# Moving eight conditioning vectors of layer 0 from the mixer's stretch to the second MLP product

## The chip, the cores and the metric

One core of a Trainium2 chip runs the whole program. The metric is the device time of one execution in microseconds (us), the median of several runs. Five engines work beside each other, each in the order of its own instruction list: TensorE (PE, products), VectorE (DVE), ScalarE (ACT), GpSimd (POOL) and SyncE (SP), which here issues every DMA transfer.

## The reference, cut to what matters

The model has two layers over 1024 latent and 128 context tokens. Each layer takes six vectors per conditioning (there are two conditionings) from one product with `w_mod`, uses two of them to scale and shift the input of the mixer, one (`g1`) to scale the mixer's result, two for the MLP's input and the last (`g2`) to scale the MLP's result:

```python
sh1, sc1, g1, sh2, sc2, g2 = ada_modulation(cond, p['w_mod'], p['b_mod'])
h = rms_norm(x, p['norm1']) * (1 + sc1) + sh1
...
x = x + g1 * mix
h2 = rms_norm(x, p['norm2']) * (1 + sc2) + sh2
x = x + g2 * (jnp.square(jax.nn.relu(h2 @ p['w1'])) @ p['w2'])
```

`ada_modulation` is `silu(cond) @ w_mod + b_mod`, a vector of 6 x 1024 numbers, which the kernel cuts into 48 tiles of 128: tiles 0 to 15 are `sh1` and `sc1`, 16 to 23 `g1`, 24 to 39 `sh2` and `sc2`, 40 to 47 `g2`.

## The kernel before, in words

Activations stand feature by feature (128 features on the partitions, tokens along the row). The program goes, for each layer, through these stages, one after the other but overlapping at the edges:

- the norm and the first input projections (in layer 0 with tiles 0 to 15 of its own vectors);
- the mixers A and B: first the RG-LRU (`rglru`, line 719, two halves of 15 steps), then the HGRN2 recurrence (`HGRN`, line 493, two head pairs of three chunks with seven levels each). Both are long chains of small operations on DVE, ACT and POOL with few products. PE fills the time with input projections, which are the "side" of each weave (lines 1477 to 1484);
- the neighbourhood attention with the rest of the projections, and the output projection;
- the first MLP product (W1) and the second one (W2, lines 1758 to 1891). W2 is done in eight groups of 8 units (`order`, `line.add`, line 1843); a unit is seven block products in a Strassen-like form, whose results DVE adds from PSUM to rows in SBUF (`second`, line 1797). POOL, ACT and DVE also cut weights and operands into a high and a low part.

A **mod tile** (`mod_tile`, line 276) makes one of the 48 tiles for both conditionings. It loads 128 x 1024 weights from `w_mod` in pieces, as wide as the buffer it is given, and has DVE multiply each piece with the silu of the conditioning and sum it along the row, once for each conditioning (line 286; the trace shows the reduction and a short read of its accumulator as two instructions). Given a buffer of 384 columns a tile takes three pieces, 3 DMAs and 6 reductions; given one of 1152 columns it takes one piece, 1 DMA and 2 reductions of 1024 columns. Tiles 8 to 15 and 32 to 39 have one short instruction more (line 292).

In layer 0 the tiles 16 to 47 are made beside the mixers: `MODS[0]`, 10 of them, between the steps of the RG-LRU, in buffers of the mixers' pool of 28 (`g_`), and `MODS[1] + MODS[2]`, 22, between the steps of HGRN2, in a pool of four buffers (`sqt`); `left` (line 1452) hands out the numbers in order. Layer 1's tiles are made under W2: 40 of them under layer 0's W2 and 8 under its own (`later`, line 1784), spread evenly over units 2 to 44 of the 64 (`MODS2`, line 51), in buffers of 1152 columns (`hr_`). `g2` is first read in the seventh group of W2, where `combine` (line 1819) multiplies by `mod[l][:, 40 + k]`.

The order on each engine is not written out: a scheduler runs a model of the program and lets each engine take the ready instruction of the highest priority. Priority follows the place in the program; the recurrences get 300 places of advance (`RG_AHEAD`, `HG_AHEAD`), the mod tiles none. An instruction that needs a buffer is ready when the buffer is free. On the chip each engine then follows the order that came out.

Of the kernel before, what the change touches and what calls it, by code (L numbers as in the profile page):

```python
# [64 lines left out]
def weave(main, n_main, side, n_side):  # L65

    done = [0, 0]
    gens = [main, side]
    n = [max(n_main, 1), max(n_side, 1)]
    live = [True, True]  # L70
    while live[0] or live[1]:
        i = 0 if live[0] and (not live[1] or done[0] * n[1] <= done[1] * n[0]) else 1
        try:
            next(gens[i])
            done[i] += 1
        except StopIteration:
            live[i] = False


def weave_steps(main, n_main, side, n_side):  # L80

    done = 0
    for i in range(n_main):
        if next(main, END) is END:
            return
        while done * n_main < (i + 1) * n_side and next(side, END) is not END:
            done += 1
        yield
    yield from main
# [20 lines left out]
def chain(*gens):  # L110
    for g in gens:
        yield from g
# [10 lines left out]
def build(ctx, tc, I, O):  # L123
# [9 lines left out]
    def urgent(gen, offset):  # L133

        while True:
            with tc.high_priority(offset):
                step = next(gen, END)
            if step is END:
                return
            yield step  # L140
# [106 lines left out]
    def load_cond(c):  # L247
        dma(sil[:, c], I["cond"][c:c + 1].to_broadcast([P, DM]))
        act(sil[:, c], sil[:, c], AF.Silu)
# [233 lines left out]
        return (M_BQ if what == "q" else M_BG) + p, e  # L483


    MODS = (10, 11, 11, 0)

    SIDE = 12 + 18 + 18
    HG_SIDE = 44
# [215 lines left out]
    def hgrns(pairs):  # L705

        rest, n = iter(()), 0
        for r in pairs:
            for g in range(NCH):
                yield from weave_steps(r.levels(g), r.LEVELS, rest, n)  # L710
                run_out(rest)
                rest, n = r.tail(g), r.TAIL
            rest, n = chain(rest, r.back()), r.TAIL + r.BACK
        yield from rest
# [94 lines left out]
    def qk_project(l, p, win, ht, qd, kd, s_, ns=range(NCH)):  # L809
        sub = vsub if p > 1 else psub  # L810
        h_t, l_t = s_("qh", F32R), s_("ql", F32R)
        yield from project(win(M_CQ + p), ht, lambda n, ps: split_q(ps, n, h_t, l_t, sub), ns)
        for j, t in enumerate((h_t, l_t)):
            for h in range(2):
                for o in range(2):
                    dma(qd[:, :, o, 2 * j + h].rearrange("t p c -> p t c"),
                        t[h * HD:(h + 1) * HD].bitcast(F32).rearrange("p (t c) -> p t c", c=P))

        def evac_k(n, ps):

            u, a, b = ft("ku"), ft("kh", F32R), ft("kl", F32R)
            w = NW if n < NCH - 1 else NW - TP
            acopy(u[:, :w].rearrange("p (i c r) -> p i r c", r=2, c=64), ps[:, :w].rearrange("p (i r c) -> p i r c", r=2, c=64))
            if n == NCH - 1:
                acopy(u[:, w:], ps[:, w:])
                dma(O["ck"][l, p * P:(p + 1) * P], u[:, w:])
            acopy(a, u)
            sub(b, u, a)
            for j, t in enumerate((a, b)):
                dma(kd[:, j, cs(n)], t.bitcast(F32))  # L830
        yield from project(win(M_CK + p), ht, evac_k, ns)
# [480 lines left out]
    for l in range(DEPTH):  # L1312
# [130 lines left out]
        def hp(p, w):  # L1443
            m, e = hgrn_evac(l, p, bp[p], w)
            return project(win(m), ht, e)

        def mods(n, piece):
            for j in take(left, n):
                mod_tile(0, j, piece)
                yield  # L1450

        left = iter(range(16, 48 if l == 0 else 16))

        def evac_vb(i, ps):
            n, j = divmod(i, 3)
# [5 lines left out]
        def v_project(g):  # L1461
            c = slice(g * 2 * P, (g + 1) * 2 * P)

            def e(i, ps):
                s = ft("vs")[:, :2 * P]
                (acopy if i % 2 else vcopy)(s, ps)
                if i < NC - 1:

                    dst = vd[ti(i), c].rearrange("(c r) m -> r c m", r=2)
                    for r in range(2):  # L1470
                        dma(dst[r], s[r * 64:(r + 1) * 64])
                else:
                    dma(vd[TS:, c], s)
                    dma(O["cv"][l][:, c], s)
            return project_tokens(l, 1 + g, ht, e, s_)

        side = chain(project_tokens(l, 0, ht, evac_vb, s_), *(hp(0, w) for w in "fbqg"))
        weave(weave_steps(urgent(chain(*(rglru(l, i, xa[i], gel[i], gw, ud, g_) for i in range(2))), RG_AHEAD), 2 * RG_STEPS,
                          mods(MODS[0], g_), MODS[0]), 2 * RG_STEPS, side, 21)
        side = chain(*(hp(1, w) for w in "fbqg"), *(v_project(j) for j in range(2)),  # L1480
                     *(qk_project(l, p, win, ht, qd[p], kd[p], s_) for p in range(3)))
        n = sum(MODS[1:3])
        weave(weave_steps(urgent(hgrns([HGRN(l, p, bp[p], ud, g_) for p in range(2)]), HG_AHEAD), HG_STEPS, mods(n, sqt), n), HG_STEPS,
# [153 lines left out]
        last = l + 1 == DEPTH  # L1637
# [95 lines left out]
        n = 0  # L1733
# [47 lines left out]
            run_out(group_operands(s))  # L1781
        for c in range(2):
            load_cond(c)
        later = iter([(1, j) for j in (range(40, 48) if last else range(40))])
        n_later, n = (8 if last else 40), 0

        rows = [row_("row") for _ in range(KD)]
        xs = [row_segs(r) for r in rows]
# [221 lines left out]
```

## Time and profile before

| what | value |
|---|---|
| median of 3 runs | 3277.85 us (3276.06 to 3279.03) |
| the profiled execution, its own time | 3276.47 us |
| its span, first to last instruction | 3274.7 us |
| granted TensorE clock over the span | 0.950 of full speed |
| PE busy | 2960.4 us, 90% of the span |
| DVE busy | 2406.1 us, 73% |
| ACT busy | 1641.4 us, 50% |
| POOL busy | 1567.8 us, 48% |
| moved by DMA | 566.48 MB, mean 173 GB/s |

The span is what lies between the first and the last instruction of the profiled execution; the execution's own time is 1.8 us more. Busy shares are averages over stages that have different limits, so a stage has to be looked at by itself. The two layers run the same code with the same shapes, but for the mod tiles: layer 1 makes none in its mixers and 8 instead of 40 in its W2. So each stage of layer 1 shows what that of layer 0 would be with fewer of them.

### The profile page before, as it was taken

The page shows a single profiled execution, that of the slowest core. Times are in us where ns is not written, and L with a number is a line of the kernel's source. Part 1 is how long each engine was busy: PE and PEld are TensorE (multiplying, and loading weights), DVE is VectorE, ACT ScalarE, POOL GpSimd, SP SyncE. Part 2 cuts the span into 40 slices and gives each one's busy share as a digit, 9 for nine tenths or more (in the row PEclk, how much of TensorE's full clock was granted, in tenths as well). Part 3 has the DMA queues.
Part 4 walks back from the last instruction along what each step waited for, and adds up shares of the span by engine and source line. Part 5 has one row for each costly group of instructions (what it writes and reads, how often), then busy time and mean ns, then how long its engine had stood idle before and what let it go on. Part 6 is the DMA issues. An engine that isn't in the chain of part 4 may idle for free. (4 is left out here: it accounts for less than half of the span.)

```text
span 3274.7 us, 61327 instructions
## 1 busy us (share of the span) xinstructions
PE 2960.4 (90%) x21208; PEld 2815.3 (86%) x21208; DVE 2406.1 (73%) x5283; ACT 1641.4 (50%) x4079; POOL 1567.8 (48%) x1528
## 2 busy tenths in 40 slices
PE   7888998998889998988868999999987999899995
PEld 7878888798789998888858889988977999899994
DVE  8899974667885568998874677346779755777787
ACT  5543234565566666344454533345646566654443
POOL 4541132345676665554545311334556765654453
PEclk8989999999899998999979999999998999999997
DMA  7342447983455567675522102689634655855552
GB/s 270 91 108 87 132 121 224 283 269 103 158 176 185 177 212 279 216 245 198 181 94 74 58 29 80 183 239 293 220 127 148 194 179 181 281 204 173 185 194 68
DMA packets 391318, 566.48 MB, mean 173 GB/s; under 512 B 45920, under 2 KB 250848, under 8 KB 391008
## 3 DMA queue, kind: packets, MB, share of 16 engines
q1 hardware_dynamic: 391008, 562.57, 53.8%
q8 instruction: 167, 2.74, 0.4%
q14 instruction: 143, 1.17, 0.1%
HBM read 397.01 MB, written 165.42 MB: 172 GB/s over the span
## 5 line engine op out<-in xcount | busy, mean ns | idle before, releaser
L189 POOL TENSOR_TENSOR wl<-wr,wh 128x512 fp32r<-128x512 f32 x164 | 231.1, 1413 | 485.4 <-ACT wh L186 379.2
L189 POOL TENSOR_TENSOR wt<-wl,wt 128x256 fp32r<-128x256 f32 x276 | 258.0, 942 | 176.5 <-ACT wt L186 116.5
L1110 PE MATMUL bB<-R,wt 128*128 128x288 f32 x768 | 236.9, 309 | 63.7 <-ACT bB L186 40.8
L189 POOL TENSOR_TENSOR ws<-wl,ws 128x512 fp32r<-128x512 f32 x160 | 227.5, 1426 | 121.4 <-ACT ws L186 121.3
L421 PE MATMUL pj<-hh,wh 128*128 128x384 f32 x640 | 223.7, 354 | 27.0 <-ACT g L213 12.3
L1110 PE MATMUL bB<-t,ws 128*128 128x288 f32 x768 | 231.7, 302 | 18.0 <-DVE hr L198 9.6
L423 PE MATMUL pj<-hh,wl 128*128 128x384 f32 x640 | 225.1, 352 | 7.1 <-POOL wl L189 7.1
L1111 PE MATMUL bB<-R,wt 128*128 128x288 f32 x768 | 231.1, 301 | 0.0
L1112 PE MATMUL bB<-R,wt 128*128 128x288 f32 x768 | 230.0, 300 | 0.0
L1111 PE MATMUL bB<-t,ws 128*128 128x288 f32 x768 | 229.6, 299 | 0.0
L1112 PE MATMUL bB<-t,ws 128*128 128x288 f32 x768 | 229.2, 299 | 0.0
L422 PE MATMUL pj<-hh,wh 128*128 128x384 f32 x640 | 223.4, 350 | 0.0
L1110 PEld LDWEIGHTS bB<-R,wt 128*128 128x128 f32 x768 | 148.2, 193 | 74.2 <-ACT bB L186 48.3
L186 ACT CAST wt<-wl 128x256 fp32r<-128x256 f32 x288 | 115.9, 406 | 159.8 <-PE bB L1112 82.0
L421 PE MATMUL wo<-u,wh 128*128 128x288 f32 x512 | 160.1, 314 | 17.1 <-DVE x L210 13.4
L1110 PEld LDWEIGHTS bB<-t,ws 128*128 128x128 f32 x768 | 147.6, 192 | 22.0 <-DVE hr L198 11.4
L186 ACT CAST wh<-wr 128x512 fp32r<-128x512 f32 x164 | 101.1, 618 | 129.3 <-PE pj L422 65.2
L207 POOL TENSOR_SCALAR pl<-pl,rc 128x384 f32<-128x384 f32 x128 | 79.1, 618 | 176.5 <-DVE rc L952 83.9
L1110 PE MATMUL bA<-R,wt 128*128 128x288 f32 x512 | 156.0, 305 | 8.1 <-DVE row L210 5.8
L1112 PE MATMUL bA<-t,ws 128*128 128x288 f32 x512 | 155.4, 304 | 8.0 <-DVE ws L192 6.5
L1110 PE MATMUL bA<-t,ws 128*128 128x288 f32 x512 | 155.1, 303 | 4.3 <-ACT ws L186 2.3
L1111 PE MATMUL bA<-R,wt 128*128 128x288 f32 x512 | 154.6, 302 | 0.0
(363 smaller groups left out, 11364.9 us busy)
## 6 DMA issues: line engine op xcount, KB each, us to landing
wr<-in_w SPq DMA_DIRECT2D x304, 256.0 KB, 3.3
R<-od SPq DMA_DIRECT2D x96, 576.0 KB, 5.6
xb<-or SPq DMA_DIRECT2D x128, 288.0 KB, 4.2
wm<-in_w_mod SPq DMA_DIRECT2D x64, 512.0 KB, 5.6
od<-sil SPq DMA_DIRECT2D x96, 288.0 KB, 2.9
od<-pad SPq DMA_DIRECT2D x96, 288.0 KB, 3.1
wr<-in_w_in SPq DMA_DIRECT2D x104, 256.0 KB, 3.0
bi<-in_bias SPq DMA_DIRECT2D x96, 192.0 KB, 4.5
```

The lines of the kernel that those rows point to most:

```text
L186: nc.scalar.copy(out=out, in_=in_)
L189: nc.gpsimd.tensor_tensor(out=out, in0=a, in1=b, op=ALU.subtract)
L207: nc.gpsimd.tensor_scalar(out=out, in0=a, scalar1=s1, scalar2=s2, op0=op0, op1=op1)
L421: mm(ps, lhsT=wh(k), rhs=ah(k), start=k == first, stop=False)
L422: mm(ps, lhsT=wh(k), rhs=al(k), start=False, stop=False)
L423: mm(ps, lhsT=wl(k), rhs=ah(k), start=False, stop=k == last)
L1110: mm(ps, lhsT=w[:, 0, ti(i)], rhs=t[:, 0], start=start and i == 0, stop=False, skip_group_check=True)
L1111: mm(ps, lhsT=w[:, 0, ti(i)], rhs=t[:, 1], start=False, stop=False, skip_group_check=True)
L1112: mm(ps, lhsT=w[:, 1, ti(i)], rhs=t[:, 0], start=False, stop=i == n - 1, skip_group_check=True)
```

## The change

`MODS[0]` falls from 10 to 2, so in layer 0 only tiles 16 and 17 stand between the steps of the RG-LRU, and tiles 18 to 39 between those of HGRN2. Tiles 40 to 47 of layer 0, which are `g2`, go to the head of the list that W2 of layer 0 works off; that list now has 48 tiles over the same 42 units. Layer 1's program is untouched, and so are the due times.

```diff
-    MODS = (10, 11, 11, 0)
+    MODS = (2, 11, 11, 0)
...
-        left = iter(range(16, 48 if l == 0 else 16))
+        left = iter(range(16, 40 if l == 0 else 16))
...
-        later = iter([(1, j) for j in (range(40, 48) if last else range(40))])
-        n_later, n = (8 if last else 40), 0
+        later = iter([(1, j) for j in range(40, 48)] if last else [(0, j) for j in range(40, 48)] + [(1, j) for j in range(40)])
+        n_later, n = (8 if last else 48), 0
```

## Rows read from the trace of the kernel before

**Rows 1.** The page: engines over the whole span, and two of the 40 slices' lines.
```profile
PE 2960.4 (90%) x21208; PEld 2815.3 (86%) x21208; DVE 2406.1 (73%) x5283; ACT 1641.4 (50%) x4079; POOL 1567.8 (48%) x1528
...
PE   7888998998889998988868999999987999899995
...
DVE  8899974667885568998874677346779755777787
```

**Rows 2.** Windows by stage: start:end, length, busy of each engine (instructions), clock, DMA share.
```profile
117.30:480.30 363.00, 322.15 (x2282) 293.80 (x2283) 334.76 (x951) 138.05 (x307) 108.96 (x103) 0.95 0.37 102
480.30:794.80 314.50, 293.13 (x2259) 264.52 (x2259) 187.02 (x555) 165.94 (x510) 124.76 (x180) 0.96 0.74 224
...
1241.70:1602.30 360.60, 329.83 (x2345) 323.01 (x2345) 329.12 (x629) 165.62 (x414) 187.92 (x171) 0.97 0.67 227
...
1758.50:2058.90 300.40, 280.59 (x2067) 254.88 (x2065) 205.35 (x555) 127.12 (x278) 86.35 (x84) 0.96 0.18 50
2058.90:2402.80 343.90, 328.97 (x2475) 298.18 (x2477) 187.80 (x555) 179.79 (x541) 142.56 (x200) 0.99 0.75 224
...
2845.40:3170.40 325.00, 316.47 (x2327) 313.93 (x2327) 241.01 (x485) 165.29 (x411) 158.48 (x168) 0.99 0.58 198
```

**Rows 3.** Tiles gr and av, layer 0: ns min/median/max, first and last start.
```profile
L740 PE MATMUL gr<-xc,gw x24: 484/486/590, 117.3 to 184.5; 128*128 128x384 f32 x24
...
L992 PE MATMUL av<-ptc,vc x256: 272/273/476, 553.9 to 794.8; 128*64 128x128 f32 x128
```

**Rows 4.** Windows of line 286 alone (the mod tiles), DVE busy, layer 0.
```profile
100.00:420.00 320.00, 132.29 (x384) 0.95 0.37 106
...
1260.00:1540.00 280.00, 114.89 (x160) 0.96 0.66 224
```

**Rows 5.** Lines by form, DVE, 100 to 420 and 1240 to 1560 us: the reductions.
```profile
L286 DVE CUSTOM_DVE_ANT_0 junk<-wm,sil,ma 128x384 bf16<-128x384 f32 x64 | 47.2, 738 | 3.6 <-DMA wm<-in_w_mod 2.8
L286 DVE CUSTOM_DVE_ANT_0 junk<-wm,sil,ma 128x256 bf16<-128x256 f32 x64 | 38.8, 606 | 0.7
...
L286 DVE CUSTOM_DVE_ANT_0 jk<-wm,sil,par 128x1024 bf16<-128x1024 f32 x80 | 114.2, 1428 | 3.8 <-ACT sil L213 2.2 <-DMA wm<-in_w_mod 1.5
```

**Rows 6.** Windows inside the mixers: RG-LRU and most of HGRN2, layers 0 and 1.
```profile
117.30:234.00 116.70, 91.50 (x493) 82.72 (x493) 103.75 (x222) 55.55 (x100) 53.76 (x46) 0.91 0.35 85
234.00:424.00 190.00, 176.15 (x1367) 162.36 (x1368) 184.83 (x593) 58.73 (x142) 36.01 (x36) 0.97 0.36 111
...
1758.50:1859.00 100.50, 85.39 (x465) 77.39 (x465) 50.09 (x83) 56.36 (x101) 50.35 (x46) 0.93 0.14 34
1859.00:2003.00 144.00, 139.29 (x1087) 126.87 (x1088) 109.70 (x325) 50.70 (x124) 24.85 (x28) 0.96 0.18 56
```

**Rows 7.** Tiles wm and scA in layer 0, and DVE's timeline around 224 us.
```profile
L286 DVE CUSTOM_DVE_ANT_0 junk<-wm,sil,ma x128: 453/605/1669, 119.5 to 416.1; 128x384 bf16<-128x384 f32 x64, 128x256 bf16<-128x256 f32 x64
...
L541 DVE COPY_PREDICATED scA<-masks,sc x42: 568/584/598, 245.4 to 480.3; 128x384 f32<-128x384 uint8 x42
...
225.72 0.61 DVE L286 CUSTOM_DVE_ANT_0 junk<-wm,sil,par 128x384 bf16<-128x384 f32 x1
```

**Rows 8.** Waits of SP, 100 to 240 us: total, times, longest.
```profile
SPq L216 <- DVE mod L286: 13.1, 4, 9.7
```

**Rows 9.** W2 of layer 0 while its mod tiles run: window, PE's and ACT's waits.
```profile
1263.00:1530.00 267.00, 237.33 (x1662) 231.37 (x1661) 259.68 (x492) 114.03 (x288) 141.31 (x121) 0.96 0.67 228
...
PE bB L1110 <- ACT bB L186: 21.0, 15, 2.4
...
ACT bB L186 <- DVE row L198: 31.1, 23, 3.7
```

**Rows 10.** Tile xm, 1200 to 1700 us: the first readers of g2.
```profile
L210 DVE SCALAR_TENSOR_TENSOR row<-row,mod,xm x16: 338/1097/1682, 1567.5 to 1620.3; 128x128 f32<-128x128 f32 x8, 128x1024 f32<-128x1024 f32 x8
```

**Rows 11.** Lines by form, POOL: W2 of layer 0 (1263:1530), then layer 1 (2867:3071).
```profile
L189 POOL TENSOR_TENSOR wt<-wl,wt 128x256 fp32r<-128x256 f32 x80 | 89.6, 1132 | 30.3 <-ACT wt L186 23.9 <-DVE mod L286 2.7 <-DVE wt L192 2.1
...
L189 POOL TENSOR_TENSOR wt<-wl,wt 128x256 fp32r<-128x256 f32 x71 | 59.3, 838 | 57.9 <-ACT wt L186 34.3 <-DVE row L198 16.5 <-issue 2.3
```

## The prediction, made before the changed kernel was built

> **What bounds the kernel now.** I first read the page's busy shares and slices [rows 1]: PE is at 90% of the span, yet its digits fall to 8 and below in many slices; DVE is at 73%, but of the six slices in which it reaches 9 five lie in two stretches, slices 3 to 5 (164 to 409 us) and 17 and 18 (1310 to 1474 us). There layer 0's mod tiles run [rows 4]. So I cut the span into stages at events that both layers have and compared the layers [rows 2, 3]: the mixers from the first gate product to HGRN2's last masked copy, the attention up to its last value product, W2 from its first product to the last plain add of its block bA. What the reader is to see: layer 0's mixers take 363.0 us and layer 1's 300.4, 62.6 more for 32 mod tiles; the attention after them takes 314.5 against 343.9, 29.4 less; W2 takes 360.6 with 40 tiles and 325.0 with 8, 35.6 more. PE does about the same products in either W2 (2345 and 2327 records), but in layer 0's mixers it does 2282 against 2067: while DVE holds up the recurrence, PE runs ahead through the projections, and gets that back in the attention. The lasting price of the 32 tiles is 62.6 - 29.4 = 33.2 us.
>
> Then I asked in each stage whether DVE is full. In HGRN2 it is busy 184.83 of 190 us (97%), in the RG-LRU 103.75 of 116.7 (89%), against 50.09 of 100.5 and 109.70 of 144 in layer 1 [rows 6]. In W2, while the mod tiles run, it is busy 259.68 of 267 us (97%), and PE's longest wait is for ACT's copy to the bank bB, which itself waits for DVE's adds to the rows [rows 9]. Both places, the one the tiles leave and the one they go to, are bound by DVE.
>
> **The change, part by part.**
>
> *Eight tiles fewer in the mixers.* 32 tiles keep DVE busy for 132.29 us [rows 4], 4.13 each, so eight take 8 x 4.13 = 33.1 us of DVE, and 24 DMAs. SP waited 13.1 us in the RG-LRU for reductions that free a buffer [rows 8]; weight loads stand behind such a wait, so fewer of these transfers can only help there.
>
> How much comes back? At the recurrence's end I take 1:1: with DVE at 97% each microsecond less of DVE is one less of stage. This needs the later tiles to move forward into the RG-LRU. The text puts eight fewer there, but the tiles of HGRN2 may run ahead of their place: the last reduction starts at 416.1, while they are spread in the text to the end of HGRN2, whose last masked copy is at 480.3 [rows 7]. I expect them to fill the RG-LRU's idle DVE in the same way. The recurrence then ends 33 us earlier. Next in line is PE: it has run less far ahead, so part returns as projections left for the attention. Of 62.6 us layer 0 got back 29.4, so 33.2 / 62.6 = 0.53 lasts, and 0.53 x 33.1 = 17.5 us. The bounds: nothing is given back, 33.1; or each tile is worth the mean of 32, 8 x 33.2 / 32 = 8.3. Lower still is the rival below in which the tiles don't move forward. A loss here I exclude: no instruction is added.
>
> *Eight tiles more under W2.* 40 tiles take 114.89 us of DVE there [rows 4], 2.87 each, so eight cost 23.0 us; a tile is cheaper by 1.26 us because two reductions of 1024 columns (1428 ns) take the place of four of 384 and two of 256 (738 and 606 ns) [rows 5]. DVE is left 7.3 us idle in 267 [rows 9], most of it at the edges; I let 1 us be absorbed. PE has no other work in W2 to run ahead with: a bank must be added to its row before it is written again. So nothing is given back later, and I take 22 us. The bounds: by the mean over the 32 tiles by which the layers differ it would be 8 x 35.6 / 32 = 8.9 us; by POOL's part (next) 23 + 6 = 29. I am near the upper one, because the row that holds is the 97%, not the mean over tiles of which the first ones filled idle time.
>
> *POOL beside these reductions.* POOL's low-part subtractions of 128x256 take 1132 ns in layer 0's W2 and 838 in layer 1's [rows 11]: 80 x 0.294 = 23.5 us more of POOL, with about 65 reductions more beside it, some 0.36 us each. Sixteen reductions would add 5.8 us to POOL, which is busy 141.31 of 267 us [rows 9] and has that free. I count it at nothing; if the weights that it makes were late, PE would wait by those 6 us.
>
> The Trainium skill speaks against the change here (SBUF — State Buffer, Who interferes with whom): a DVE instruction with two inputs in SBUF and a GpSimd one that reads SBUF share a port, and the second one blocks until the first has ended. By that rule, with every one of the 16 reductions holding POOL for its 1.43 us and all of it reaching PE, the time would be 3282 + 23 = 3305. The trace agrees in direction [rows 11], but shows 0.36 us for each, which POOL's idle time covers, and so 3282.
>
> *Moved with it.* Eight DMAs of 512 KB (three pieces become one) pass to W2, in SP's queue and in the ring of buffers that also feeds the operands. The DMA engines are 0.67 busy there [rows 2], so 4.2 MB find room: nothing, and some us of operand wait if a buffer is late. `g2` is first read at 1567.5 [rows 10], after all mod tiles (their last reduction is before 1540 [rows 4]), and its tiles come first in the list: no new wait. Layer 1's 40 tiles follow within the same units.
>
> **The sum** against the profiled execution's own 3276.5 us: - 17.5 + 22 = 3281.0. The runs' median, 3277.85, is 1.4 above that execution, so 3282.4 us, slower by 0.14%. A measurement of this kernel can tell some 0.2%, 6.6 us, from no change: below 3271.3 is faster, above 3284.4 slower.
>
> **The rivals**, on the scale of the median.
>
> *1. W2 pays, the mixers hardly return: slower.* The place is HGRN2 from 234 us on. If the scheduler doesn't bring its tiles forward, RG-LRU with 2 tiles gets nearly as short as layer 1's: 8/10 of 116.7 - 100.5, 13 us. But tile 11 starts at 225.7 in the kernel before [rows 7], so about two of the 22 were done when HGRN2 began; now they would stand in it with DVE full, 8 to 10 us. 13 - 10 = 3, of which 0.53 lasts: 2 us. With 22 of W2 that is + 20, 3298. It decides as soon as fewer than about 4 tiles move forward. For: the priorities follow the text, and none of HGRN2's tiles ran before the first ten were done. Against: the ten left no room, and later the tiles did run ahead. 0.2.
>
> *2. The mixers return all: faster.* The tail of the DVE-full stretch is what the last tiles cost; if 24 tiles leave PE as little idle as layer 1's mixers do (19.8 us against 40.9 [rows 2]), nothing is given back: - 33.1 + 22, 3266.8. For: the price per tile must rise with their number, and 33.2 us are just eight tiles at 4.13. Against: layer 1's attention is 29.4 us longer. 0.17.
>
> *3. W2 costs its mean price only:* - 17.5 + 8.9, 3269.3. Against: DVE's 97%. 0.05.
>
> *4. POOL becomes W2's bound,* and the weights' low parts come late: + 6, 3288. For: it is slowed already. Against: before these subtractions it is idle for 30.3 us, mostly waiting for ACT [rows 11]. 0.13. The Trainium skill's port rule (SBUF — State Buffer, Who interferes with whom) would make this rival likelier and dearer, up to the 3305 above, which the 0.36 us don't bear out.
>
> *5. The change doesn't do what it says:* the scheduler rearranges so much that the places of the tiles don't matter. 0.03, anywhere in the range.
>
> **How the numbers follow.** The likeliest case, 17.5 back and 22 paid, has 0.42 and gives 3282. Within 0.2% are it, nearly all, and little else: 0.42 in all, as what it loses at its edges it gets from the others. Slower: rivals 1 and 4 and a share of 5, 0.36. Faster: rivals 2 and 3, 0.22. For 8 in 10 the range goes from a little under rival 2, 3264, to rival 1, 3298; it takes in both bounds of the mixers with 22 paid (3267 and 3291.6) and leaves out only combinations of two extremes. The likeliest case alone would lie between 3274 (25 back, halfway to the upper bound, and 22 paid) and 3288 (13 back, halfway to the mean price, and 23 paid).
>
> **What would show it.** In the changed profile: reductions on buffers of 384 columns 144 instead of 192, busy near 99 us; reductions of 1024 columns 112 instead of 96. The mixers' stage near 330 us and the attention's near 330, with the last small reduction near 383; W2's near 383, with DVE at 97% or more while its tiles run and PE still waiting for the copy to bB. Wrong would be: a mixers' stage that stays over 350 (rival 1), an attention that stays at 315 (rival 2), a W2 under 372 (rival 3) or PE waiting for POOL's weights in it (rival 4).

## The result and the profile after

The changed kernel takes 3300.11 us (median of 6 runs, 3291.68 to 3301.31) against 3276.06 us of the kernel before in the same set: 1.0079 of it, 95% interval 1.0066 to 1.0093, so 26 us slower by this ratio (24 by the two medians). That is outside the predicted range, 2 us above its upper end, and 18 us above the predicted time. The profiled execution took 3298.01 us, its span is 3296.2 us.

The page of the kernel after, the lines that answer to [rows 1]:

```profile
PE 2966.8 (90%) x21208; PEld 2818.2 (85%) x21208; DVE 2405.4 (73%) x5219; ACT 1646.8 (50%) x4083; POOL 1563.7 (47%) x1528
...
PE   7888999999799988888869899999987999899995
...
DVE  8799864577975578999893587345778755777787
```

DVE's total is the same within a microsecond, though eight tiles now cost 22 us where they cost 33: other DVE instructions became longer. Its slices show where the tiles went: the fifth and sixth fell from 9 and 7 to 8 and 6, and the 9s of W2 now reach from the 17th to the 19th, one more than before.

The windows of the same stages, kernel after (first gate product to HGRN2's last masked copy, to the attention's last value product, W2 to its last plain add of bA, from there to layer 1's first gate product); they answer to [rows 2]:

```profile
118.20:471.00 352.80, 313.55 (x2231) 285.28 (x2231) 304.90 (x854) 140.13 (x303) 101.45 (x97) 0.96 0.33 89
471.00:790.80 319.80, 300.89 (x2308) 271.23 (x2310) 187.59 (x555) 169.39 (x518) 130.47 (x186) 0.97 0.75 226
1236.40:1634.70 398.30, 346.26 (x2390) 336.21 (x2390) 368.49 (x675) 170.36 (x423) 190.91 (x176) 0.94 0.66 223
1634.70:1782.70 148.00, 115.29 (x660) 111.86 (x659) 103.45 (x236) 68.95 (x164) 67.93 (x54) 0.84 0.31 105
```

The mixers' stage lost 10.2 us against [rows 2], not 33, and the attention took 5.3 of them back. W2 grew by 37.7 us and the stretch behind it shrank by 8.2 (156.2 before), because the last plain add of bA, which ends the one and begins the other, moved behind other work (2390 products stand before it, where 2345 did); so I read these two as one from here on: 546.3 us, against 516.8 before.

The reductions stand where they were foreseen: 144 on buffers of 384 columns, 112 of 1024 columns in the whole program, and in layer 0's W2 96 of 1405 ns with 7.5 us of accumulator reads, 142.4 us against 120.4 (114.2 [rows 5] and 6.2 of reads): 22.0 us more of DVE. In the view of [rows 4], which counts overlapping instructions once, it is 135.70 against 114.89, 20.8 us. The tiles' place is as predicted, their price is not.

### The profile page after: what moved, and what is told of

Its sections match the earlier page's. It is cut to its first block, busy times and chain, and to the rows that moved or that the text cites. A ratio compares the mean times of both kernels' runs of the same rounds, so it can differ in the third digit from the quotient of the medians.

```text
span 3296.2 us, 61231 instructions
## 1 busy us (share of the span) xinstructions
PE 2966.8 (90%) x21208; PEld 2818.2 (85%) x21208; DVE 2405.4 (73%) x5219; ACT 1646.8 (50%) x4083; POOL 1563.7 (47%) x1528
## 5 line engine op out<-in xcount | busy, mean ns | idle before, releaser
L1110 PE MATMUL bA<-R,wt 128*128 128x288 f32 x512 | 157.9, 308 | 5.5 <-DVE row L198 4.2
L286 DVE CUSTOM_DVE_ANT_0 jk<-wm,sil,par 128x1024 bf16<-128x1024 f32 x112 | 156.6, 1398 | 8.4 <-DMA wm<-in_w_mod 4.6
```

The lines of the kernel that those rows point to most:

```text
L286: nc.vector.tensor_tensor_reduce(out=junk[:, :w], in0=r[:, :w], in1=sil[:, c, k0:k0 + w], scale=1.0, scalar=acc[c], op0=ALU.mult, op1=ALU. ...
L1110: mm(ps, lhsT=w[:, 0, ti(i)], rhs=t[:, 0], start=start and i == 0, stop=False, skip_group_check=True)
```

## The experiments

The first three runs separate the two halves of the change and measure the tiles' full price.

**e1_w2_only**: the mixers as before, `g2` computed twice.

```diff
-        later = iter([(1, j) for j in (range(40, 48) if last else range(40))])
-        n_later, n = (8 if last else 40), 0
+        later = iter([(1, j) for j in range(40, 48)] if last else [(0, j) for j in range(40, 48)] + [(1, j) for j in range(40)])
+        n_later, n = (8 if last else 48), 0
```

> The mixers stay as in the kernel before; W2 makes the eight tiles of g2 a second time, so it has the 48 tiles of the changed kernel. This is the price of the W2 part alone. By the prediction: +22 us against the kernel before. By the theory formed from the two traces (the eight tiles cost their own 22 us of DVE, and some 8 us more because the weight subtractions of 128x256 beside them take longer): +28 to +30 us, W2 at 395 to 400 us against 360.6. By the mean price per tile (rival 3): +9 us.

Measured: 1.0036 (1.0023 to 1.0049), +12 us; W2 375.6 and the stretch behind it 156.3, 531.9 us together. By the runs, 7 to 16 us, the prediction's +22 and the +28 to +30 missed, and only the mean price of +9 fits; by the stages 22.0 us of DVE became some 14 us of time, half of what the changed kernel pays.

**e2_mixers_only**: `MODS = (2, 11, 11, 0)`, tiles 16 to 39, and instead of tiles 40 to 47

```diff
+    nc.vector.memset(mod[0][:, 40:48], 0.5)
```

> The mixers lose the eight tiles of g2 as in the changed kernel, and nothing takes their place: g2 is a constant set by one memset, so these eight tiles of the vectors are left out of the computation, and W2 keeps its 40 tiles. By the prediction: -17.5 us against the kernel before. By the theory formed from the two traces (from 380 us on PE is full, so the tiles' end brings the end of the recurrence forward by only some 10 us, of which half is given back): -5 to -8 us. By rival 2 (all returned): -33 us.

Measured: 1.0032 (1.0019 to 1.0045), +10 us; mixers 353.1, attention 319.5, W2 and the stretch behind it 520.4 us. No theory expected a loss. The profiled execution was the shortest of this kernel (3272.36 us, median 3281.78), so its stages show less than the runs do; some 3 us of the loss stand in W2, whose order changed a little, the rest I can't place. By the runs the two halves, +12 and +10, would make 22 us together; the stages further down say otherwise for the mixers.

**e3_no_tiles**: `MODS = (0, 0, 0, 0)`, no tile in the mixers, memsets for tiles 16 to 47.

> All 32 mod tiles of layer 0's mixers are left out (tiles 16 to 47 are constants set by memsets), everything else as in the kernel before. It measures what the 32 tiles cost in all, which the prediction took from the difference of the two layers, 62.6 - 29.4 = 33.2 us. If the step from the layers was right: -33 us, mixers near 300 us, attention near 344 us; and with -5 to -8 us for the first eight removed the price per tile would rise with fewer tiles. If the layers differ for other reasons too (PE makes 215 more products in layer 0's stage): -15 to -25 us, eight tiles being a quarter of it.

Measured: 0.9926 (0.9907 to 0.9945), -24 us. Windows of mixers and attention:

```profile
116.60:412.90 296.30, 274.42 (x2062) 249.64 (x2060) 205.73 (x556) 128.70 (x278) 81.86 (x82) 0.97 0.19 51
412.90:753.10 340.20, 328.76 (x2484) 298.48 (x2482) 189.43 (x555) 181.03 (x543) 143.53 (x201) 0.99 0.73 226
```

Together 636.5 us, against 677.5 before: the layers' difference of 33 us was a fair size for all 32, if a little small. But W2 with the stretch behind it took 527.3 us, 10 more than before, with the same text and the same 40 tiles. That was the first sign that W2's time does not follow from its text.

**c0_before_again**: the kernel before, as a control.

> The kernel before, unchanged, as a control: it says how far the profile of one execution and a set of runs can be trusted, since the kernel without the eight tiles measured 1.0032 of the kernel before although its profiled execution was 4.5 us shorter. If a set of runs separates kernels to about 0.15%: a ratio between 0.9985 and 1.0015, and a profile whose stages agree with those shown of before within some 5 us each.

Measured: 1.0003 (0.9988 to 1.0018). Its windows:

```profile
118.50:478.60 360.10, 322.28 (x2282) 294.21 (x2283) 333.83 (x951) 138.11 (x307) 108.94 (x103) 0.96 0.37 103
478.60:791.00 312.40, 291.18 (x2258) 262.70 (x2259) 186.78 (x555) 165.88 (x510) 124.40 (x180) 0.97 0.75 226
1238.20:1599.30 361.10, 326.46 (x2345) 319.43 (x2345) 331.02 (x630) 165.16 (x414) 189.76 (x171) 0.98 0.66 227
1599.30:1755.70 156.40, 117.26 (x705) 112.41 (x704) 111.25 (x251) 72.51 (x173) 75.28 (x60) 0.88 0.33 115
```

Mixers and attention 672.5 us (677.5 in the first profile), W2 with the stretch behind it 517.5 (516.8): the mixers repeat to 5 us, W2 to 1. Layer 1, whose DVE order the change leaves alone, took 1509.7 and 1516.2 us, so a whole-span difference of 6 us in one profile says nothing.

Next, the mixers: is it the number of tiles, or where they run?

**e5_place**: again 24 tiles and `g2` a constant, but `MODS = (10, 7, 7, 0)`.

> Again 24 of the 32 tiles in the mixers and g2 a constant (its eight tiles are left out of the computation), but the eight are taken from HGRN2's share, not from the RG-LRU's: ten tiles stand between the steps of the RG-LRU and 14 in HGRN2. If the number of tiles decides: the same as without the eight of the RG-LRU, +8 to +11 us against the kernel before by the runs. If what cost there was that the RG-LRU got ahead of its projections or that HGRN2 ran as full as before (rival 1): less than the kernel before, -5 to -15 us.

Measured: 1.0011 (0.9994 to 1.0028). Mixers 349.1, attention 319.8: 668.9 us, some 5 less than with the change's places; W2 with its stretch 528.6, 11 more than before. What the mixers returned, W2 took. Neither expectation holds: the +4 us (-2 to +9) lie between them.

**e6_sixteen**: `MODS = (2, 7, 7, 0)`, tiles 32 to 47 constants.

> Sixteen of the 32 tiles are left out of the mixers (tiles 32 to 47 are constants): 2 between the steps of the RG-LRU, 14 in HGRN2. Without 8 the runs gave about +9 us, without all 32 about -24 us. By the prediction's 0.53 x 4.13 us per tile: -35 us. If the first eight removed only rearrange the stage and the rest pays by the piece: about halfway, -5 us; if HGRN2's fullness is what costs (here it has eight fewer of its own): -15 to -20 us.

Measured: 0.9975 (0.9963 to 0.9988), -8 us; mixers 332.4, attention 330.9 (663.3 together), W2 with its stretch 527.2. Of the expectations the halfway one, -5, fits (the interval is -12 to -4); -15 to -20 and -35 don't.

**e8_attention16** and **e9_attention24**: 16 and 24 tiles put into the attention's steps, `MODS = (2, 7, 7, 0)` and `(2, 3, 3, 0)`; the line that makes them in the first:

```diff
-            run_out(take(ahead, LOADS[1]))
+            run_out(take(ahead, LOADS[1])); [mod_tile(0, j, sqt) for j in take(late, steps(16, (8, 26), i))]
```

> Sixteen tiles (32 to 47) leave the mixers and are made beside the attention, spread over its steps 8 to 26, in buffers of 384 columns; W2 as in the kernel before in the text, but in the scheduler's other order, which cost some 10 us with the 16 tiles left out. In the attention DVE is busy 187 of 315 us, so 16 x 4.13 = 66 us find room by the sum. If room is all that counts: -8 us against the kernel before, as with the tiles left out. If reductions between the softmax steps delay PE's next products: attention 10 to 30 us longer, the kernel 0 to +20 us.

> Twenty-four tiles (24 to 47) leave the mixers for the attention, steps 8 to 28; the mixers keep eight. The price per tile in the mixers was about 0.1 us for the first eight taken away, 1.3 for the next eight and 1.7 for each of the last sixteen (mixers and attention together). If the 99 us of DVE find room in the attention: mixers and attention together near 650 us against 674, the kernel -10 to -15 us with W2's dearer order. If not: the attention over 360 us and no gain, 0 to +15 us.

Measured: 1.0044 (1.0028 to 1.0059) and 1.0048 (1.0030 to 1.0066). Neither theory was tested, for the tiles did not go there. The line of the small reductions in the run with 16 (last start at 442.6 us, the attention begins at 482.3):

```profile
L286 DVE CUSTOM_DVE_ANT_0 junk<-wm,sil,ma x128: 465/605/1516, 119.4 to 442.6; 128x384 bf16<-128x384 f32 x64, 128x256 bf16<-128x256 f32 x64
```

The scheduler ran them ahead into the mixers, whose stage was 365.0 us as with 32 tiles (364.0 in the run with 24, last start at 443.4 us). A tile that depends on nothing but a free buffer runs when DVE has a gap, wherever it stands in the text.

Then W2's order.

**e10_other_order**: the change with `MODS = (10, 7, 7, 0)` in place of `(2, 11, 11, 0)`, and nothing else.

> The change once more, with the eight tiles taken from HGRN2's share (MODS 10, 7, 7) instead of the RG-LRU's. In W2 it computes what the changed kernel does, 48 tiles at the same places in the text, but the scheduler's order for DVE there is the one of the kernel that only repeats g2 in W2, and not the one of the changed kernel. If the order that the scheduler happens to find decides half of W2's price: W2 and the stretch after it take 532 us together as in that kernel, not 546, and the kernel is +8 to +11 us against the kernel before (-5 from the mixers, +15 from W2) instead of +25. If W2's price goes by the tiles alone: +20 to +25 us.

Measured: 1.0027 (1.0015 to 1.0039), +9 us, as the order's theory had it. Windows as above:

```profile
117.20:467.00 349.80, 313.31 (x2231) 284.96 (x2231) 308.96 (x854) 135.48 (x299) 101.68 (x97) 0.95 0.32 89
467.00:789.60 322.60, 302.54 (x2308) 272.55 (x2310) 187.49 (x555) 170.50 (x518) 131.78 (x186) 0.97 0.75 224
1234.30:1607.40 373.10, 333.33 (x2343) 323.38 (x2342) 353.54 (x664) 166.94 (x413) 187.83 (x170) 0.97 0.68 231
1607.40:1765.10 157.70, 118.89 (x709) 115.04 (x709) 111.23 (x249) 72.19 (x174) 75.49 (x61) 0.87 0.33 115
```

W2 with its stretch: 530.8 us, 1.1 from e1_w2_only, whose DVE list in W2 is the same instruction for instruction, and 15.5 below the changed kernel, which makes the same 48 tiles at the same places in the text. DVE's is not the only list that differs between the two: PE's, ACT's and POOL's in W2 do too, while in e1_w2_only all four are those of this run. So these runs show the price of an order, and not of one engine's list.

**e11_w2_last**: as e1_w2_only, with the eight repeated tiles at the end of the list.

> The mixers as in the kernel before, g2 a second time in W2 as in the run on W2 alone, but at the end of the list instead of at its head: the same work in W2 (two short instructions of layer 1's tiles come earlier), in a third order. If each order has its own price: W2 with the stretch after it anywhere from 525 to 546 us, reproducible, the kernel +8 to +29 us. If W2's price goes by the work alone: 532 us and +12 us, as with the tiles at the head.

Measured: 1.0047 (1.0031 to 1.0063), +15 us; 533.7 us. A third order of the same work, at nearly the second one's price; so this run does not separate its two expectations.

**c1_after_again**: the changed kernel once more.

> The changed kernel again, as a control: whether its W2 with the stretch after it takes 546 us in every execution or in the profiled one alone. If the scheduler's order sets it: 543 to 549 us again, PE's clock at its lower level for some 40 us of W2 as before, and +25 us against the kernel before. If the profiled execution was a bad draw: nearer the 532 us that the same 48 tiles take in the other order.

Measured: 1.0104 (1.0085 to 1.0123), +34 us. W2 and the stretch behind it:

```profile
1244.40:1638.90 394.50, 340.60 (x2391) 330.16 (x2391) 368.91 (x677) 170.25 (x424) 192.60 (x176) 0.97 0.66 226
1638.90:1785.90 147.00, 112.87 (x660) 109.54 (x659) 102.06 (x236) 69.02 (x164) 68.14 (x54) 0.85 0.30 104
```

541.5 us, a little under the 543 to 549 expected of the order: the dear W2 is the order's, not one execution's. The part about the clock fell: W2's mean granted clock was 0.97 here and 0.94 in the first profile, so about 5 of the first profile's 546.3 us were its own.

**e7_spread**: the changed kernel with W2's 48 tiles over units 2 to 60, `MODS2 if last else (2, 60)`.

> The changed kernel, with the 48 tiles of layer 0's W2 spread over units 2 to 60 instead of 2 to 44. In the kernel before DVE was busy 97% while the tiles ran, and in the last units of W2, without tiles, 73% (21.15 of 29 us) to 86% (27.37 of 32). If the price of W2 is that DVE is over-full while the tiles run: W2 shorter by some 10 to 15 us, and the kernel +10 to +15 us against the kernel before instead of +26. If the later tiles meet the final adds and the result's combination, which fill DVE at the end: no gain, +25 us or more.

Measured: 1.0067 (1.0046 to 1.0088), +22 us. W2 fell to 370.2 us, but the stretch behind it rose to 168.5: 538.7 together. The later tiles pushed the last units' adds out, as the second theory had it.

Last, other places for the tiles.

**e4_w1**: `g2` beside the first MLP product, `steps(8, (12, 28), n)` after its `line.add`, with buffers from `sqt`. (From W1 on the silus' buffer holds other data, so `g2` there is not the reference's; its instructions are.)

> The mixers lose the eight tiles as in the changed kernel, but g2 is made under the first MLP product (W1) between its units 12 and 28 in buffers of 384 columns, where from 1000 to 1200 us PE was busy all of the time and DVE 57% of it. Eight tiles are 33 us of DVE against some 80 us of free DVE. If DVE's free time is what decides: they cost nothing there, and the kernel is as fast as the one without them in the mixers (-5 to -8 us against the kernel before by the theory from the traces, -17.5 by the prediction). If the reductions disturb POOL's subtractions or the weight transfers in W1: some +5 us more, no change against the kernel before.

Measured: 1.0024 (1.0013 to 1.0036), +8 us. Mixers and attention 673.1, W1 450.9 (446.9 before), W2 with its stretch 521.8. W1 takes eight tiles for 4 us, the cheapest place found, but the mixers had returned nothing to pay for it.

**e14_held8**, **e12_held16**, **e13_held24**: 8, 16 and 24 tiles in the attention (`MODS = (10, 7, 7, 0)`, `(2, 7, 7, 0)` and `(8, 0, 0, 0)`), in one buffer of 384 columns that is freed with the mixers' buffers, so that they can't run ahead; the edit of the first:

```diff
-                (("ks", 3, KW), ("ck", 3, 2 * CTX), ("vc", 2, CTX), ("q", 3, 4 * P), ("pc", 6, CTX), ("ut", 4, P))}
+                (("ks", 3, KW), ("ck", 3, 2 * CTX), ("vc", 2, CTX), ("q", 3, 4 * P), ("pc", 6, CTX), ("ut", 4, P), ("wm", 1, NW))}
...
-            run_out(take(ahead, LOADS[1]))
+            run_out(take(ahead, LOADS[1])); [mod_tile(0, j, pool["wm"]) for j in take(late, steps(8, (8, 26), i))]
```

> Only the eight tiles of g2 held back for the attention (ten stand in the RG-LRU, 14 in HGRN2), with W2's order on DVE exactly that of the kernel before. So the mixers' part is seen without any change in W2. Leaving out these eight brought mixers and attention together 5.6 us in the profile. If W2's order is what hid it in the runs: -5 us, and 0 to -5 us if the attention pays for the tiles. By the prediction's 17.5 us for eight: -17 us.

> Sixteen tiles (32 to 47) in the attention again, but in a buffer of their own that comes free only when the mixers' buffers do, so that the scheduler can't run them ahead into the mixers. W2 in the text as before, its order on DVE the one of the kernel with eight tiles left out. If the place where the tiles run decides what they cost: mixers near 332 us as with these 16 left out, against 365 where the same tiles ran ahead; W2 with the stretch after it near 520 us; and if the attention takes the 66 us of DVE without a delay, the kernel at -5 to -10 us. If the reductions delay the attention by more than 10 us: no gain or slower.

> Twenty-four tiles (24 to 47) held in the same way, eight are left in the mixers, where no tile then stands in HGRN2. If HGRN2 pays by how long its first half shares DVE with tiles: mixers near 300 to 305 us, the attention 340 us or more, both together 640 to 650 us against 674. W2's order on DVE is a fourth one, its price unknown within 0 to +12 us. So -30 to -10 us where the attention hides the 99 us of DVE, and slower than the kernel before where it is prolonged by 40 us or more.

Measured: 1.0037 (1.0024 to 1.0051), 1.0101 (1.0083 to 1.0120) and 1.0319 (1.0303 to 1.0336). The mixers did what place demands: 350.6, 332.7 and 304.0 us. But the attention took 337.2, 358.8 and 377.8, and W1 443.7, 455.7 and 542.0, for the tiles of the two larger runs reached into it. In e14_held8 DVE stood 27.7 us behind the single buffer in the attention, with the softmax queued after it:

```profile
DVE junk L286 <- DMA wm<-in_w_mod: 27.7, 17, 8.1
```

So this is a test of a single buffer as much as of the place. W2 with its stretch was 518.8 us in e14_held8, where DVE's list there is exactly that of the kernel before. No variant that does all the work of the kernel before was faster than it.

The sums by W2's order on DVE (W2 + the stretch behind it, then mixers + attention, us). The shares say, roughly, how many of DVE's instructions in W2 stand in the same sequence as in the kernel before:

| order of W2 | tiles there | runs | W2 + stretch |
|---|---|---|---|
| that of before | 40 | before, c0, e14 | 516.8, 517.5, 518.8 |
| 95% the same | 40 | e2, e4, e12 | 520.4, 521.8, 520.1 |
| 66% the same | 40 | e13 | 520.3 |
| another (57% the same) | 40 | e3, e5, e6, e8, e9 | 527.3, 528.6, 527.2, 523.7, 527.7 |
| of e1 | 48 | e1, e10 | 531.9, 530.8 |
| of e11 | 48 | e11 | 533.7 |
| of e7 | 48 | e7 | 538.7 |
| of the changed kernel | 48 | after, c1 | 546.3, 541.5 |

| tiles in the mixers | runs | mixers + attention |
|---|---|---|
| 32 | before, c0, e1, e11 | 677.5, 672.5, 673.5, 674.7: mean 674.6 |
| 32, of which 16 or 24 stand in the attention's text | e8, e9 | 682.3, 681.9 |
| 24 (2 and 22) | after, c1, e2, e4, e7 | 672.6, 675.7, 672.6, 673.1, 676.0: mean 674.0 |
| 24 (10 and 14) | e5, e10 | 668.9, 672.4 |
| 16 | e6 | 663.3 |
| 0 | e3 | 636.5 |

The changed kernel's account is then -0.6 us in mixers and attention and 543.9 - 517.7 = +26.2 in W2 and the stretch behind it, 25.6 in all; measured 26 and, in the second set, 34. The runs of e2_mixers_only, +10 us without any tile added, don't fit the first of these figures. But the profiled executions of the changed kernel, c1, e4 and e7 lie within some 3 us of their kernels' medians and show 672.6 to 676.0 us for mixers and attention, where 32 tiles take 672.5 to 677.5. So a loss in the mixers' half is unlikely, and 7 of e2's 10 us stay open.

## Why the prediction was wrong

**The mixers: 17.5 us predicted, 0.6 found.** The tiles did move forward, as the forecast needed and rival 1 denied. Line 286 in the kernel before and after, RG-LRU and HGRN2:

```profile
117.30:234.00 116.70, 56.92 (x135) 0.91 0.35 85
234.00:420.00 186.00, 74.74 (x248) 0.97 0.37 111
```

```profile
118.20:234.00 115.80, 45.66 (x114) 0.93 0.36 79
234.00:420.00 186.00, 56.13 (x172) 0.97 0.31 93
```

The RG-LRU, given 2 tiles instead of 10, still did four fifths of its reductions, and HGRN2 18.6 us fewer. What failed is the step "At the recurrence's end I take 1:1: with DVE at 97% each microsecond less of DVE is one less of stage". The last small reductions now start at 374.7 instead of 416.1 [rows 7], 41 us earlier; the last masked copy comes only 9 us earlier:

```profile
L286 DVE CUSTOM_DVE_ANT_0 junk<-wm,sil,ma x96: 465/607/1704, 120.3 to 374.7; 128x384 bf16<-128x384 f32 x48, 128x256 bf16<-128x256 f32 x48
...
L541 DVE COPY_PREDICATED scA<-masks,sc x42: 565/584/605, 242.9 to 471.0; 128x384 f32<-128x384 uint8 x42
```

Between the two lie the windows that decide it, before and after:

```profile
380.00:400.00 20.00, 20.00 (x181) 19.24 (x180) 19.69 (x72) 4.55 (x11) 0.00 (x0) 1.00 0.43 119
400.00:420.00 20.00, 20.00 (x146) 19.75 (x146) 19.13 (x53) 5.95 (x14) 6.01 (x7) 1.00 0.43 137
```

```profile
380.00:400.00 20.00, 19.46 (x175) 18.49 (x173) 12.30 (x37) 4.87 (x14) 0.00 (x0) 1.00 0.29 79
400.00:420.00 20.00, 20.00 (x161) 18.95 (x162) 13.46 (x36) 5.87 (x15) 4.25 (x4) 1.00 0.25 74
```

Before, PE and DVE were both full. After, DVE falls to 25.8 of 40 us and PE stays at 39.5. Of the 14.2 us in which DVE now stands between 380 and 420 us, 12.7 are waits for products of PE; the longest of them in total, which the kernel before does not have there, is the masked copies':

```profile
DVE scA L541 <- PE sc L536: 7.5, 3, 2.6
```

So it was PE, with its projections, that the recurrence waited for here, and DVE was full of tiles only because they filled its gaps. In this stretch (25th to 29th masked copy) the recurrence took 39.5 us instead of 44.9 (42.0 and 45.0 in c1 and c0); further back, where tiles still ran, it kept its pace (102.5 instead of 105.6 us from the first copy to the 21st). So the tiles at the end of the list were nearly free, and the price is in the first ones: the eight removed returned 0.6 us, the next eight 10.7, the last sixteen 26.8 (single profiles of this stretch repeat to 5, and the places count too: eight taken from HGRN2's share returned some 4). The mean that I took as lower bound (8.3) was above the truth.

The step "0.53 lasts" failed too. By the means of the runs with 32 tiles and with the change's 24 the mixers became 8.5 us shorter and the attention 7.9 longer: 0.93 went back. PE is busy for the same time in the two stages together, 615.3 us before and 614.4 after, and what it no longer did of its projections in the mixers it had to do in the attention.

A smaller miss: "weight loads stand behind such a wait, so fewer of these transfers can only help". SP's waits for reductions, 100 to 240 us, kernel after:

```profile
SPq L216 <- DVE ma L286: 29.2, 15, 5.2
SPq L216 <- DVE mod L286: 10.2, 6, 5.2
```

39.4 us, against 25.6 before (the 13.1 of [rows 8] and 12.5 for the tile `ma`): HGRN2's tiles have four buffers, not 28, and pulled into the RG-LRU they hold SP. Its waits for the recurrence's `r` got shorter by 20 us, though, and all its waits together went only from 106 to 111 us. With ten tiles left there (e5, e10) the reductions' part is 24 to 25 us again, and the mixers' stage some 4 us shorter (349.1 and 349.8 against 353.9); that the one causes the other is not shown.

**W2: 22 predicted, 26 found, for another reason.** The 22 us of DVE were about right (20.8 to 22.0). What failed is the step from them to time, "nothing is given back later, and I take 22": it let 1 us be absorbed, and the sum had no term for another order of W2's other instructions. The same reductions cost 13 to 16 us in the orders of e1, e10 and e11 and 24 to 29 in the changed kernel's. The windows above say how. From the control to e10_other_order DVE's busy time in W2 and the stretch behind it rose from 442.3 to 464.8 us (22.5), and its idle time fell from 75.2 to 66.0: the tiles filled 9 us of gaps, and 13 remained. In the changed kernel it rose to 471.9, since other instructions became longer too, and 74.4 us stayed idle: nothing was filled.

PE's columns of these windows show where the time lies. PE makes the same products in all of them (3050 to 3052 records). In the control it is busy for 443.7 us and stands for 73.8; in e10_other_order for 452.2 and 78.6; in the changed kernel for 461.6 and 84.7, in its second run for 453.5 and 88.0. So 10 to 18 of the changed kernel's 24 to 29 us above the control are the same products taking longer, and 11 to 14 are waits; of e10's 13 they are 8 and 5. The longer products go with the clock: over both windows together it is 0.95 in the control, 0.94 in e10 and c1 and 0.92 in the first profile of the changed kernel. (The first profile of the kernel before has 447.2 and 69.6, so a few us of the busy time differ from execution to execution.)

The waits are longer in the changed kernel's order, above all those for row adds. PE's largest wait from W2's start to the last tiles, kernel after, its second run, and e10_other_order:

```profile
PE bB L1110 <- ACT bB L186: 30.7, 14, 4.4
```

```profile
PE bB L1110 <- ACT bB L186: 30.2, 13, 4.4
```

```profile
PE bB L1110 <- ACT bB L186: 21.5, 15, 3.0
```

Waits of 2.2 us in the mean instead of 1.4, 9 us more than in e10_other_order. The control has waits of 1.5 us:

```profile
PE bB L1110 <- ACT bB L186: 25.4, 17, 3.3
```

(In the kernel before it is 23.3 us, 16 times, up to 1530 us; the 21.0 of [rows 9] are those up to about 1520.) One of the changed kernel's, on DVE's timeline; that the others came about in the same way is not shown:

```profile
1373.68 1.27 DVE L192 TENSOR_TENSOR wt<-wr,wt 128x256 fp32r<-128x256 f32 x1
...
1376.71 1.27 DVE L286 CUSTOM_DVE_ANT_0 jk<-wm,sil,par 128x1024 bf16<-128x1024 f32 x1
...
1377.91 1.94 DVE L192 TENSOR_TENSOR R<-xb,R 128x576 fp32r<-128x576 f32 x1
1379.77 0.45 DVE L198 TENSOR_TENSOR z<-bE,z 128x288 f32<-128x288 f32 x1
1380.14 0.44 DVE L198 TENSOR_TENSOR row<-bB,row 128x288 f32<-128x288 f32 x1
1380.51 0.41 DVE L192 TENSOR_TENSOR wt<-wr,wt 128x256 fp32r<-128x256 f32 x1
```

and PE's:

```profile
1377.42 0.29 PE L1112 MATMUL bC<-R,wt 128*128 128x288 f32 x1
1381.05 0.61 PE L1110 MATMUL bB<-R,wt 128*128 128x288 f32 x1 [3.34 <-ACT bB L186]
```

The row add that frees bB stands behind a reduction of 1.27 us and an operand subtraction of 1.94; ACT's copy starts when it ends, at 1380.62, and PE stands for 3.34 us. In e10_other_order no wait for bB is longer than 3.0 us. Why the scheduler's model finds the one or the other order was not tried.

**What was right.** POOL at nothing, rival 4 out: its subtractions took 1016 ns while the tiles ran, against 1132 [rows 11], and PE waited 0.9 us in all for one of them, up to 1566 us. The Trainium skill's rule of the shared port (SBUF — State Buffer, Who interferes with whom), by which I had worked out 3305, is near the measured time, but not by its own way: e10_other_order avoids half of the loss in W2 with as many reductions beside POOL. The trace does agree with the rule itself: in the timeline above the same 128x256 subtraction takes 1.27 us at 1373.68, while POOL runs one of its own from 1372.83 for 1.84 us, and 0.41 us at 1380.51, with POOL idle since 1379.23.

**The rivals.** Rival 1's time, 3298, is close, with its first half for another reason (the tiles moved forward, but what they left was not the bound). The sign that was named for it, a mixers' stage over 350 us, came all the same (352.8), so that sign did not mark its mechanism. The mechanism that decided, the scheduler's order, was rival 5, which I gave 0.03 and no price. It has one now: 6 to 11 us for 40 tiles, 8 to 16 for 48, and a change in the mixers is enough to trigger it. That the measured time lies 2 us from rival 1's is luck.

## What to carry to other kernels

An engine that is 97% busy with work that only fills its gaps is not a bound: look whether a second engine is full in the same window, and price the last pieces of such work by what happens where they end, not by the mean over all of them. Where a scheduler writes the order, a change moves instructions far from its own place; compare the lists of instructions, stage by stage, and measure a variant that does the same work in another order before a difference of 10 us is put down to the work. A stage that ends earlier beside a full engine can give the time back in the next one.

## What the hardware showed unexpectedly

After the stall above PE did not come back at full speed. Windows of the kernel after around it, the granted clock in the third column from the end:

```profile
1374.00:1376.00 2.00, 2.00 (x16) 1.90 (x16) 2.00 (x3) 1.80 (x5) 1.71 (x3) 1.00 0.89 313
...
1380.00:1382.00 2.00, 0.95 (x4) 0.95 (x5) 2.00 (x6) 0.38 (x1) 0.00 (x0) 0.50 0.52 145
1382.00:1384.00 2.00, 2.00 (x10) 2.00 (x10) 1.89 (x5) 0.70 (x2) 0.32 (x1) 0.50 0.72 268
1384.00:1387.00 3.00, 3.00 (x16) 3.00 (x15) 2.30 (x4) 0.41 (x1) 1.20 (x2) 0.57 0.64 187
1387.00:1390.00 3.00, 3.00 (x24) 3.00 (x24) 2.65 (x6) 0.88 (x3) 0.73 (x1) 1.00 0.51 188
```

The clock is at 1.00 (2.4 GHz) up to the stall of 3.34 us and at 0.50 (1.2 GHz) for the products behind it, 10 in 2 us instead of 16, before it returns: by an estimate from these windows, some 5.5 us at half the clock, the wait of 3.3 us cost PE 2 to 3 us more after its end. The two profiles of the changed kernel differ in how long the clock was at 0.50 in W2: worked out from the mean clocks, 0.944 and 0.967, it was some 45 us of 398 in the first and some 26 of 395 in the second.
